# Two queues for the first half of x, and a broadcast copy on two engines, in a two-layer decoder trunk

## The chip, the cores and the metric

The kernel runs on one core of a Trainium2 chip. The time is that of one execution on the device, in microseconds (us). The core has five engines with an instruction stream of their own: PE (TensorE, matrix products), DVE (VectorE), ACT (ScalarE), POOL (GpSimd) and SP (SyncE, which here only issues transfers). PEld is PE's loading of weights. Transfers between the chip's memory (HBM) and the core's SBUF run on 16 DMA engines; an engine that issues one puts it into its own queue and goes on.

## The reference: what is computed

One sequence of 1024 tokens, 1024 wide, goes through two layers and a last norm. Each layer computes

```
mod   = silu(c) @ ada_w[layer] + ada_b[layer]          # shift, scale, gate
h     = rmsnorm(x, norm_g) * (1 + scale) + shift
x     = x + gate * mixer(h)
```

with `rmsnorm(x, g) = x * rsqrt(mean(x*x) + 1e-6) * g` per token. Layer 0's mixer is an input projection, eight heads of sliding-window attention beside eight heads of forgetting attention, a SiLU gate and an output projection. Layer 1's is a projection, a causal convolution of width 4, a gated linear recurrence along the tokens, a SiLU gate and an output projection. The result is `rmsnorm(x, final_g)`. All is float32.

## The kernel before, in words

The kernel keeps x transposed: the 1024 features lie as 8 blocks (k = 0 to 7) of 128 partitions, the tokens along the free dimension, in two halves of 512. For a matmul in float32r each operand is split into a high part (a rounded copy, made by ACT) and a low part (the rest, made by POOL), and a product is three matmuls: high by high, low by high, high by low. Names with `hh`, `whi` are high parts, `hlo`, `wlo` low ones; `ws` are the split weights of the first projection, both parts.

Nearly every instruction goes through a small class, `Queue` (L75), so that the profile gives the helper's line, L85, for all of them; the tiles' names tell them apart. Where an engine's name stands in the set `ordered`, its instructions keep the order in which the program writes them; elsewhere a scheduler orders them. From `ordered |= ALL` (L415) on, the opening is in written order.

The opening, which the change touches:

- SyncE issues `col` (all the small vectors), then x of the first half in five pieces (`load_x(0)`: k = 0-1, 2-3, 4-5 of 512 KB each, then 6 and 7 of 256 KB each), then the rows of `ada` for the shifts and scales and the weights `wg` of the first five gate tiles (`load_block`).
- ACT, DVE and POOL make silu(c) from `col`; POOL spreads it along the free dimension (`vb8`), and PE transposes it into `crow_ps`. ACT loads a table of functions at the start, and another ahead of the square roots.
- `squares(0)`: ACT squares blocks 0, 2, 4, 6 and 7, in this order; DVE squares 1, 3 and 5 and sums pairs (POOL one of them). `norm_sums` adds over the partitions with matmuls against ones (`psq`). Between them PE is given matmuls that compute nothing (`warm`).
- `rstd_of` (L255) makes 1/sqrt of the mean for each token. At that point token t of group i stands on partition t, column i (`v`). The factors have to lie along the tokens on every partition, so they are copied to 128 columns each (`vb`) and PE transposes those blocks of 128 x 128 (`rs`).
- For each of 8 blocks k: two dot products on DVE give the block's scale and shift (`mod_first`), DVE multiplies x by rs and the scale, ACT adds the shift twice (once rounded to `hh`), POOL takes the difference (`hlo`), and PE runs 15 matmuls with the five gate tiles (`pst`): ten with hh, five with hlo. During block 7 ACT also splits `raw_gate`, the weights of a sixth gate tile.

After that comes the rest of layer 0, then layer 1. At the very end the final norm is done for tokens 0 to 511, 512 to 767 and 768 to 1023 in turn; only the last of the three has no matmul left beside it. There `rstd_of` is used again, the transposed factors are also copied by ACT to SBUF (`rsb`) for POOL, and DVE and POOL multiply and SyncE stores.

Of the kernel before, what the change touches and what calls it, by code (L numbers as in the profile page):

```python
# [12 lines left out]
F32 = mybir.dt.float32  # L13
# [11 lines left out]
P = 128  # L25
S = 1024
D = 1024
KT = D // P
HALF = 512
# [19 lines left out]
def hybrid_trunk(  # L49
# [23 lines left out]
    ordered = set()  # L73
# [25 lines left out]
    act, dve, gp = Queue("act", nc.scalar), Queue("dve", nc.vector), Queue("gp", nc.gpsimd)  # L99
# [3 lines left out]
    def copy(out, in_, scale=1.0):  # L103
        act.activation(out, in_, AF.Copy, scale=scale)
# [41 lines left out]
    gp.memset(tiny, 1e-30)  # L146
    tiny2 = const.tile([P, 1], F32, name="tiny2")
    col = const.tile([P, NCOL], F32, name="col")
    sync.dma_start(col, cols)
    nsink = const.tile([P, 8], F32, name="nsink")  # L150
    bfb = const.tile([P, 8], F32, name="bfb")

# [18 lines left out]
        sub(dve, out, l, c)  # L171


    cact = const.tile([P, KT], F32, name="cact")
    ce = const.tile([P, KT], F32, name="ce")
    act.activation(ce, col[:, C_C : C_C + 8], AF.Exp, scale=-1.0)
# [2 lines left out]
    mul(dve, cact, ce, col[:, C_C : C_C + 8])  # L179
    act.activation(tiny2, cact[:, 0:1], AF.Exp)  # L180
    act.activation(tiny2, tiny2, AF.Sqrt)


    l0 = ctx.enter_context(ExitStack())
    gyp = l0.enter_context(tc.tile_pool(name="gyp", bufs=2, reuse_waits="tile"))
    l0a = ctx.enter_context(ExitStack())
    at = l0a.enter_context(tc.tile_pool(name="at", bufs=2, reuse_waits="tile"))

# [3 lines left out]
    def t4(tag, name, dt=F32, bufs=None):  # L192
        bufs = bufs or BUFS[tag]
        return at.tile([P, 1024], dt, tag=tag, name=name, bufs=bufs)

    xh = []
    for h in range(2):
        t = gyp.tile([P, KT, HALF], F32, tag="gy", name=f"x_{h}")
        xh.append(t)

    mm = pe.matmul

# [32 lines left out]
    def norm_sums(sq, w, name, ps=None):  # L235

        psq, steps = sum_steps(sq, w, name, ps)
        for f in steps:
            f()
        return psq  # L240
# [11 lines left out]

        return psq, [lambda n=n, i=i: step(n, i) for n in range(len(sq)) for i in range(w // P)]

    def rstd_of(psq, w, pool, tags, name, ps=None):  # L255

        nt = w // P

        v, t = (psq[:, i * P : i * P + 2 * nt] for i in (1, 2))
        y = pool.tile([P, 8], F32, tag="ny", name=f"ny_{name}", bufs=2)[:, : 2 * nt]  # L260
        dve.tensor_scalar(out=v, in0=psq[:, 0 : 2 * nt], scalar1=1.0 / D, scalar2=EPS, op0=ALU.mult, op1=ALU.add)
        act.activation(y, v, AF.Sqrt)
        dve.reciprocal(y, y)

        dve.scalar_tensor_tensor(out=t, in0=v, scalar=-0.5, in1=y, op0=ALU.mult, op1=ALU.mult)
        mul(dve, t, t, y)
        dve.scalar_tensor_tensor(out=v, in0=t, scalar=1.5, in1=y, op0=ALU.add, op1=ALU.mult)
        vb = pool.tile([P, nt, P], F32, tag=tags[0], name=f"vb_{name}", bufs=2)
        dve.tensor_copy(vb, v.rearrange("p (i two) -> p i two", two=2)[:, :, 0:1].to_broadcast([P, nt, P]))

        def spread():
            prs = (ps or ps_t)(f"rs_{name}")
            for i in range(nt):
                tp(prs[:, i * P : (i + 1) * P], vb[:, i])
            if ps:
                return prs
            rs = pool.tile([P, w], F32, tag=tags[1], name=f"rsb_{name}", bufs=2)
            copy(rs, prs[:, :w])
            return rs, prs

        return spread
# [90 lines left out]
    def start_w(i, k):  # L372
        return tuple(t[:, k % 2, i] for t in four[k // 2]) if i < 4 else tuple(t[:, k] for t in one)

    def load_x(h):
        for k0, k1 in ((0, 2), (2, 4), (4, 6), (6, 7), (7, 8)):
            sync.dma_start(xh[h][:, k0:k1], xT[:, h, k0:k1])

    hl_ada = {}

    parts = {}
# [31 lines left out]
        return sq[0:KT:2]  # L413

    ordered |= ALL  # L415
    load_x(0)
    for c in range(4):
        load_block(c)
    vb8 = at.tile([P, KT, P], F32, tag="P", name="vb8", bufs=NP)
# [13 lines left out]
    psq = norm_sums(sq, HALF, "n0_0", ps_s)  # L433
    mod_first(0, 1)
    warm(WARM)
    spread = rstd_of(psq, HALF, at, ("ptl", "pth"), "n0_0", ps_s)
    mod_first(0, 0)
    split_start(0)
    prs = spread()
# [1115 lines left out]
    for t0, tw in ((0, 512), (512, 256), (768, 256)):  # L1555
# [29 lines left out]
            act.activation(sqs[1], xn[:, KT - 1], AF.Square)  # L1585
        for e in range(KT):
            act.activation(xn[:, e], xn[:, e], AF.Copy, scale=col[:, C_FG + e : C_FG + e + 1])
        spread = rstd_of(norm_sums(sqs, tw, f"n2_{t0}"), tw, xp, ("vb", "rsb"), f"n2_{t0}")
        rs, prs = spread()
        for e in range(KT):  # L1590
            mul(*((gp, xn[:, e], xn[:, e], rs) if e % 4 == 3 else (dve, xn[:, e], xn[:, e], prs[:, :tw])))
# [77 lines left out]
```

## Time and profile before

| what | value |
| --- | --- |
| median of 3 runs | 882.5 us (881.85 to 883.75) |
| profiled execution | 882.07 us, span 880.3 us |
| PE, PEld busy | 857.9, 728.0 us |
| DVE, ACT, POOL busy | 561.5, 536.9, 385.6 us |
| mean granted PE clock | 0.990 |
| first x issue to first projection matmul | 1.19 to 17.03 us |
| last projection matmul group of the opening | 44.33 us |
| last residual add to the last store issue | 869.52 to 874.86 us (first of four stores) |

The span runs from the first to the last instruction; the time around it, 1.8 us, is not in the trace. In a row of the timeline stand the start and the duration in us, the engine, the operation, the tile written and the tiles read, and in brackets how long the engine had been idle and what it waited for. A start is measured from the span's start. SPq and ACTq are the issues of transfers by SyncE and ACT.

### The profile page before, as it was taken

The numbers are of one execution on the slowest core, as the hardware profiler recorded it, in microseconds if no ns is written. First come the engines' busy times: TensorE is split into PE (matmuls) and PEld (weight loads), VectorE is DVE, ScalarE is ACT, GpSimd is POOL, SyncE is SP. The second block draws the span as 40 slices with busy tenths as digits, with TensorE's granted clock in tenths as the row PEclk, the third lists the DMA queues.
The fourth block names the chain that finished last, engine by engine and source line by source line (L and its number), as shares of the span: only waits on it lengthen the run. The fifth ranks groups of instructions, "written<-read, shape, count | busy, mean of one in ns | idle before, by whom it ended". The sixth has DMA issues, their size and how long they took to land.

```text
span 880.3 us, 13493 instructions
## 1 busy us (share of the span) xinstructions
PE 857.9 (97%) x4618; PEld 728.0 (83%) x4618; DVE 561.5 (64%) x1134; ACT 536.9 (61%) x1047; POOL 385.6 (44%) x429
## 2 busy tenths in 40 slices
PE   9999999999989999999999999999999999989995
PEld 8787898888878888888877888878888877868995
DVE  7886657688676566666656668375667655563643
ACT  5765124788685566666666647357767876673532
POOL 4843222334342232232664655532775556585100
PEclk9999999999999999999999999999999999989998
DMA  9944772100113223322373564411221211226042
GB/s 344 403 180 127 218 237 63 47 18 24 37 43 115 87 87 123 123 87 79 118 232 106 176 209 146 141 63 54 79 78 55 71 55 65 86 83 215 14 145 81
DMA packets 54620, 103.83 MB, mean 118 GB/s; under 512 B 6960, under 2 KB 20720, under 8 KB 54040
## 3 DMA queue, kind: packets, MB, share of 16 engines
q1 hardware_dynamic: 53400, 101.93, 35.1%
q10 hardware_dynamic: 1152, 1.05, 0.4%
q8 instruction: 36, 0.59, 0.3%
q14 instruction: 32, 0.26, 0.1%
HBM read 94.02 MB, written 8.93 MB: 117 GB/s over the span
## 4 chain that ended last, share of the span: by engine, by line
PE 77%; issue 6%; POOL 5%; DMA 4%; DVE 3%; ACT 3%; SPq 0%; POOLq 0%; DVEq 0%; ACTq 0%
PE ps_fill L85 23%; PE ps_o L85 10%; PE ps_lx L85 6%; PE pst L85 6%; PE ps_o0c L85 5%; PE ps_lg L85 5%; PE oB L85 4%; PE sB L85 4%; PE ptB L85 4%; PE ps_v L85 3%; DMA ada<-in_ada_dram 2%; PE sA L85 2%; PE oA L85 1%; POOL wlo_lg L85 1%; PE ptA L85 1%
## 5 line engine op out<-in xcount | busy, mean ns | idle before, releaser
L85 PE MATMUL ps_o<-y1h,wo 128*128 128x256 f32 (+1 forms) x336 | 75.2, 318 | 0.0
L85 DVE TENSOR_TENSOR ptl_B<-ptB,pth_B 128x512 fp32r<-128x512 f32 (+1 forms) x80 | 50.9, 636 | 34.7 <-ACT pth_B L85 33.9
L85 ACT ACTIVATE pB<-pB,mnB 128x128 f32<-128x128 f32 (+3 forms) x64 | 49.6, 775 | 32.7 <-DVE mnB L85 26.8
L85 ACT ACTIVATE pth_B<-ptB 128x512 fp32r<-128x512 f32 (+1 forms) x80 | 44.1, 551 | 41.1 <-PE ptB L85 40.2
L85 DVE SCALAR_TENSOR_TENSOR xc_r<-ps_lx,col,xc_r 128x509 f32<-128x509 f32 (+2 forms) x48 | 35.7, 745 | 43.4 <-ACT xt_r L85 42.2
L85 POOL TENSOR_SCALAR_AFFINE_SELECT pB<-pB 128x128 f32<-128x128 f32 x64 | 18.6, 293 | 95.8 <-DMA pB<-gd 88.8
L85 PEld LDWEIGHTS ps_o<-y1h,wo 128*128 128x128 f32 x336 | 56.0, 190 | 4.4
L85 PE MATMUL pst<-hh,ws 128*128 128x512 f32 x192 | 55.5, 397 | 0.0
L85 PE MATMUL ps_o<-y1l,wo 128*128 128x256 f32 (+1 forms) x168 | 53.7, 320 | 0.0
L85 PE MATMUL ps_lg<-h1h,wlo_lg 128*128 128x512 f32 x128 | 50.2, 392 | 0.9 <-POOL wlo_lg L85 0.8
L85 PE MATMUL ps_lx<-h1l,whi_lx 128*128 128x512 f32 x128 | 50.3, 393 | 0.2 <-POOL h1l L85 0.2
L85 PE MATMUL ps_lx<-h1h,wlo_lx 128*128 128x512 f32 x128 | 50.3, 393 | 0.2
L85 PE MATMUL ps_lx<-h1h,whi_lx 128*128 128x512 f32 x128 | 50.3, 393 | 0.0
L85 PE MATMUL ps_lg<-h1l,whi_lg 128*128 128x512 f32 x128 | 49.9, 390 | 0.0
L85 PE MATMUL ps_lg<-h1h,whi_lg 128*128 128x512 f32 x128 | 49.8, 389 | 0.0
L85 POOL TENSOR_TENSOR wlo_lx<-raw_lx,whi_lx 128x512 fp32r<-128x512 f32 x16 | 30.6, 1930 | 43.3 <-ACT whi_lx L85 34.1
L85 ACT ACT_TABLE_LOAD x35 | 44.9, 1283 | 5.1 <-issue 3.0
L85 DVE CUSTOM_DVE_ANT_0 pB<-sB,pB 128x384 f32<-128x384 f32 (+2 forms) x64 | 35.4, 555 | 17.4 <-PE sB L85 10.0
L85 PE MATMUL ptB<-ident,pB 128*128 128x128 f32 x288 | 45.1, 273 | 1.2 <-DVE ptl_B L85 0.7
L85 PEld LDWEIGHTS ptB<-ident,pB 128*128 128x128 f32 x288 | 35.8, 140 | 12.1 <-PE rbT_B L85 1.5
L85 PEld LDWEIGHTS pst<-hh,ws 128*128 128x128 f32 x192 | 35.8, 188 | 9.2 <-issue 0.6
L85 ACT ACTIVATE y1h<-sg_r 128x512 fp32r<-128x512 f32 x16 | 10.0, 632 | 44.9 <-POOL sg_r L85 39.8
(312 smaller groups left out, 2853.5 us busy)
## 6 DMA issues: line engine op xcount, KB each, us to landing
ada<-in_ada_dram SPq DMA_DIRECT2D x32, 512.0 KB
x<-in_xT_dram SPq DMA_DIRECT2D x20, 256.0 KB
ada<-in_ada_dram SPq DMA_DIRECT2D x4, 1024.0 KB
pB<-gd SPq DMA_DIRECT2D x8, 512.0 KB
raw_o0a<-in_wo_dram SPq DMA_DIRECT2D x16, 256.0 KB
raw_o0c<-in_wo_dram SPq DMA_DIRECT2D x16, 256.0 KB
x1d<-x SPq DMA_DIRECT2D x16, 256.0 KB
raw_lx<-in_wl_dram SPq DMA_DIRECT2D x16, 256.0 KB
```

The lines of the kernel that those rows point to most:

```text
L85: ins = issue(*args, **kw)
```

## The change

Three edits, the first two of which belong together.

`col` and x of the first half are issued at one place at the very start, and the five pieces of x are dealt to two queues: ACT issues pieces 1 and 3 (k = 0-1 and 4-5), SyncE pieces 2, 4 and 5. ACT and SyncE keep written order over this piece of the program. The second half's x is still all SyncE's.

In `rstd_of` a new argument `two` halves the copy of the factors: DVE copies the first half of the token groups, ACT the second. It is used for the first half's norm at the opening (4 groups of 128, so 128 x 256 for each engine) and for the last 256 tokens of the final norm (2 groups, 128 x 128 each). The other norms keep the whole copy on DVE.

```
-    sync.dma_start(col, cols)
...
+    xh = [gyp.tile([P, KT, HALF], F32, tag="gy", name=f"x_{h}") for h in range(2)]
+
+    def load_x(h, queues=(sync,)):
+        for i, (k0, k1) in enumerate(((0, 2), (2, 4), (4, 6), (6, 7), (7, 8))):
+            queues[i % len(queues)].dma_start(xh[h][:, k0:k1], xT[:, h, k0:k1])
+
+    ordered |= {"act", "sync"}
+    sync.dma_start(col, cols)
+    load_x(0, (act, sync, act, sync, sync))
...
     act.activation(tiny2, tiny2, AF.Sqrt)
+    ordered.clear()
...
-    def rstd_of(psq, w, pool, tags, name, ps=None):
+    def rstd_of(psq, w, pool, tags, name, ps=None, two=False):
...
-        dve.tensor_copy(vb, v.rearrange("p (i two) -> p i two", two=2)[:, :, 0:1].to_broadcast([P, nt, P]))
+        vs = v.rearrange("p (i two) -> p i two", two=2)[:, :, 0:1]
+        cut = nt // 2 if two else nt
+        dve.tensor_copy(vb[:, :cut], vs[:, :cut].to_broadcast([P, cut, P]))
+        if two:
+            copy(vb[:, cut:], vs[:, cut:].to_broadcast([P, nt - cut, P]))
...
-    load_x(0)
...
-    spread = rstd_of(psq, HALF, at, ("ptl", "pth"), "n0_0", ps_s)
+    spread = rstd_of(psq, HALF, at, ("ptl", "pth"), "n0_0", ps_s, two=True)
...
-        spread = rstd_of(norm_sums(sqs, tw, f"n2_{t0}"), tw, xp, ("vb", "rsb"), f"n2_{t0}")
+        spread = rstd_of(norm_sums(sqs, tw, f"n2_{t0}"), tw, xp, ("vb", "rsb"), f"n2_{t0}", two=t0 == 768)
```

On SyncE, at the start of the program (x_103 and x_91 are the first half's x, before and now; rows of 128x1024 are the 512 KB pieces):

```order
 L85 DMA col<-in_cols_dram 128x144
-L85 DMA x_103<-in_xT_dram 128x1024 x3
-L85 DMA x_103<-in_xT_dram 128x512 x2
+L85 DMA x_91<-in_xT_dram 128x1024
+L85 DMA x_91<-in_xT_dram 128x512 x2
 L85 DMA ada_0_125<-in_ada_dram 128x1024 x2
```

Two of the 512 KB pieces are gone from this queue; `ada` stands two issues nearer to its head.

On ACT, from the first instruction to the split of the first weights, as it stands now (psq holds the factors, raws the weights as loaded, ws their split):

```order
L85 DMA x_91<-in_xT_dram 128x1024 x2
L85 ACT_TABLE_LOAD
L85 ACTIVATE ce<-col 128x8
...
L85 ACTIVATE sq_ptl_1_179<-x_91 128x512
L85 ACTIVATE gsc<-mod,col 128x1
L85 ACTIVATE ny_n_0_217<-psq_n_0_192 128x8
L85 ACTIVATE vb_n_0_224<-psq_n_0_192 128x256
L85 ACTIVATE ws_0_0_115<-raws_0_128 128x512
L85 ACTIVATE ws_0_123<-raw_raws_0_130 128x512
```

New here are the two issues ahead of the table load, and ACT's half of the copy (vb) between the square root (ny) and the split of the first weights. On DVE the copy at the same place is 128x256 instead of 128x512. On PE and POOL every instruction stands where it stood.

On ACT, the last instructions of the program, as they stand now:

```order
L85 ACTIVATE sq_768_9098<-x_768_8861 128x256
L85 ACTIVATE x_768_8861<-x_768_8861,col 128x256
L85 ACTIVATE ny_n_768_9113<-psq_n_768_9108 128x4
L85 ACTIVATE vb_n_768_9120<-psq_n_768_9108 128x128
L85 ACTIVATE rsb_n_768_9126<-rs_n_768_9123 128x256
```

The row vb is new; DVE's copy at this place is 128x128 instead of 128x256.

More of the change, by code (lines that the diff above doesn't have):

```diff
@@ L171, in log1p_exp_neg_abs @@
         sub(dve, out, l, c)
+    l0 = ctx.enter_context(ExitStack())
+    gyp = l0.enter_context(tc.tile_pool(name="gyp", bufs=2, reuse_waits="tile"))
+    xh = [gyp.tile([P, KT, HALF], F32, tag="gy", name=f"x_{h}") for h in range(2)]
[5 more added lines that the diff above has]
+    load_x(0, (act, sync, act, sync, sync))
     cact = const.tile([P, KT], F32, name="cact")
@@ L181, in hybrid_trunk @@
     act.activation(tiny2, tiny2, AF.Sqrt)
-    l0 = ctx.enter_context(ExitStack())
-    gyp = l0.enter_context(tc.tile_pool(name="gyp", bufs=2, reuse_waits="tile"))
+    ordered.clear()
     l0a = ctx.enter_context(ExitStack())
@@ L194, in t4 @@
         return at.tile([P, 1024], dt, tag=tag, name=name, bufs=bufs)
[L196 to L199, printed above, removed]
     mm = pe.matmul
@@ L373, in start_w @@
         return tuple(t[:, k % 2, i] for t in four[k // 2]) if i < 4 else tuple(t[:, k] for t in one)
-    def load_x(h):
-        for k0, k1 in ((0, 2), (2, 4), (4, 6), (6, 7), (7, 8)):
-            sync.dma_start(xh[h][:, k0:k1], xT[:, h, k0:k1])
     hl_ada = {}
```

## The prediction

> **What bounds the kernel now.** I read the page first, for the engine that carries the span and the chain that ended last; then busy time by stretch for the opening 60 us and the timeline of each engine there; then the last 12 us, because the change touches only these two ends.
>
> ```profile
> span 880.3 us, 13493 instructions
> PE 857.9 (97%) x4618; PEld 728.0 (83%) x4618; DVE 561.5 (64%) x1134; ACT 536.9 (61%) x1047; POOL 385.6 (44%) x429
> PE 77%; issue 6%; POOL 5%; DMA 4%; DVE 3%; ACT 3%; SPq 0%; POOLq 0%; DVEq 0%; ACTq 0%
> ```
>
> TensorE (PE) is busy for 97% of the span and is 77% of the last chain. A shift won in the opening therefore passes through the long middle as a shift, and one won behind the last matmul counts directly. The opening, by stretch (the columns are busy time of PE, PE's weight loads, VectorE, ScalarE, GpSimd, then granted clock, DMA share, GB/s):
>
> ```profile
> 1.75:2.50 0.75, 0.75 (x5) 0.75 (x5) 0.00 (x0) 0.26 (x1) 0.00 (x0) 1.00 1.11 180
> 2.50:3.50 1.00, 1.00 (x7) 1.00 (x6) 0.44 (x3) 0.21 (x1) 0.19 (x1) 1.00 0.66 143
> 3.50:8.20 4.70, 4.70 (x34) 4.70 (x34) 2.23 (x4) 3.19 (x6) 2.31 (x2) 1.00 1.02 405
> 12.60:16.00 3.40, 3.40 (x18) 3.36 (x18) 3.14 (x8) 1.22 (x3) 2.50 (x2) 0.50 1.01 376
> 16.00:45.40 29.40, 29.38 (x130) 23.31 (x129) 25.16 (x39) 21.95 (x39) 23.28 (x18) 1.00 1.04 403
> 45.40:60.00 14.60, 14.51 (x72) 11.91 (x70) 12.08 (x16) 7.76 (x13) 6.52 (x5) 1.00 0.36 142
> ```
>
> The DMA engines are full from 3.50 us on and stay at about 400 GB/s to 45.40. So two things run abreast in the opening: a stream of transfers that is never idle once it has started, and the norm chain up to the first projection matmul. Which one sets PE shows at the last of the eight blocks of projection matmuls:
>
> ```profile
> 17.03 2.60 PE L85 MATMUL pst<-hh,ws 128*128 128x512 f32 x10
> 38.73 0.63 ACT L85 ACTIVATE whi_gate<-raw_gate 128x512 fp32r<-128x512 f32 x1 [0.79 <-DMA raw_gate<-in_wt_dram]
> 40.98 0.72 ACT L85 ACTIVATE hh<-x,mod 128x512 fp32r<-128x512 f32 x1 [0.82 <-DVE x L85]
> 41.75 2.20 PEld L85 LDWEIGHTS pst<-hh,ws 128*128 128x128 f32 x10 [0.46 <-ACT hh L85]
> 44.33 1.00 PEld L85 LDWEIGHTS pst<-hlo,ws 128*128 128x128 f32 x5 [0.38 <-POOL hlo L85]
> ```
>
> PE starts the first block at 17.03. At the eighth it waits 0.46 us for hh and 0.38 us for hlo. Both are late because ScalarE (ACT) waited 0.79 us for raw_gate, a transfer, with the split of the last weights and the scale of the block queued behind it. So at 45 us the transfers have overtaken the norm chain: PE has 0.84 us of slack there against its own start, and what counts at the end of the opening is how much earlier the stream of transfers runs.
>
> **The change, part by part.** It removes no arithmetic. Two of the five x transfers of the first half move from SyncE's queue to the head of ScalarE's, and half of two copies moves from VectorE (DVE) to ACT.
>
> *Issue of x.*
>
> ```profile
> 0.73 0.40 SPq L85 DMA_DIRECT2D col<-in_cols_dram  x1
> 1.19 2.59 SPq L85 DMA_DIRECT2D x<-in_xT_dram  x5
> 3.82 0.94 SPq L85 DMA_DIRECT2D ada<-in_ada_dram  x2
> L679 ACTq DMA_DIRECT2D bias<-rd x8: 310/432/606, 129.4 to 134.2; - x8
> ```
>
> SyncE issues col at 0.73 and the first x at 1.19; five x issues take 2.59, 0.52 each. On ACT a transfer's issue takes 432 ns in the median (310 to 606; the bias transfers of this trace). In the change ACT issues the first x as its first instruction, at 0.73, which is 1.19 - 0.73 = 0.46 earlier, and its second at about 1.2. SyncE has three x left and reaches the first ada at about 1.19 + 3 x 0.52 = 2.75 instead of 3.82, so it stays ahead of the engines.
>
> How much earlier does the full stream start? Bounds: nothing, if the slow second from 2.50 to 3.50 (143 GB/s) is not made by the order of issues. At most, the stream would be full from 1.75 on: 0.75 x (1 - 180/405) + 1.00 x (1 - 143/405) = 0.42 + 0.65 = 1.06 us. I take 0.46, the offset of the issue, since the bytes behind the first x are the same and the engines are full once x flows.
>
> *When x lands, and the norm chain.*
>
> ```profile
> 5.38 0.63 ACT L85 ACTIVATE sq<-x 128x512 f32<-128x512 f32 x1
> 6.66 0.63 ACT L85 ACTIVATE sq<-x 128x512 f32<-128x512 f32 x1 [0.65 <-DMA x<-in_xT_dram]
> 7.96 0.63 ACT L85 ACTIVATE sq_pth<-x 128x512 f32<-128x512 f32 x1 [0.67 <-DMA x<-in_xT_dram]
> 8.63 1.29 ACT L85 ACTIVATE sq_ptl<-x 128x512 f32<-128x512 f32 x2
> 5.39 0.69 DVE L85 TENSOR_TENSOR sq<-x 128x512 f32<-128x512 f32 x1 [1.78 <-DMA x<-in_xT_dram]
> 10.17 0.69 DVE L85 TENSOR_TENSOR sq_ptl<-sq_ptl,sq_ptl 128x512 f32<-128x512 f32 x1
> ```
>
> The squares follow the landings: 5.38, 6.66 and 7.96 lie 1.3 apart, and 512 KB at 405 GB/s is 1.29. If the five pieces still land in their order, all is 0.46 earlier; ACT ends its squares at 9.92 - 0.46 = 9.46 and DVE's last sum begins near 9.7 in place of 10.17. If the two queues share the engines by halves, the pieces 2 (ACT), 4 and 5 (SyncE) overlap: piece 2 lands not at 7.96 - 0.46 = 7.50 but shortly before the last one, near 8.7, while the last byte of x still lands 0.46 earlier. ACT takes the squares in order, so three of them (0.655 each with the gap) then run from 8.7 to 10.65, and the last sum begins near 10.7: 0.5 later than before. So the first block starts between 0.46 earlier and 0.5 later.
>
> The Trainium skill ("DMA: Bandwidth & Descriptors", sections "Queues, rings and completion order" and "Issuing engines are not separate DMA queues") speaks for the halves, and against this change: the queues of the two engines sit on the same 16 DMA engines, which serve them in turn packet by packet, so that a second issuer saves only its time of issue. By that rule the stream still gains the 0.46 of issue, and the norm chain is the 0.5 later; no row read here shows two queues busy at once.
>
> Both cases give nearly the same end. In order: PE's own arrival at the eighth block is 41.75 - 0.46 - 0.46 = 40.83, raw_gate lands 0.46 earlier, so the block starts 0.46 earlier. By halves: PE arrives at 41.29 + 0.5 = 41.79. ACT's chain ahead of raw_gate ended at 38.73 - 0.79 = 37.94, now 38.44, so whi_gate starts 0.29 earlier and hlo with it. PE reaches the hlo matmuls at 43.95 + 0.5 - 0.46 = 43.99, finds hlo at 44.33 - 0.29 = 44.04, and is 0.29 ahead. **Term: -0.3 to -0.46; I take -0.4.** Behind it PE is busy for 14.51 of 14.60 us, and raw_gate's successors move with the stream.
>
> *ACT pays for its issues.*
>
> ```profile
> 0.73 1.28 ACT L85 ACT_TABLE_LOAD   x1 [0.73 <-PEq L1658]
> 2.75 0.21 ACT L85 ACTIVATE ce<-col 128x8 f32<-128x8 f32 x1 [0.74 <-DMA col<-in_cols_dram]
> 3.67 1.04 POOL L85 COPY vb<-cact 128x1024 f32<-128x1024 f32 x1 [0.70 <-DVE cact L85]
> 6.12 1.04 PE L85 MATMUL crow_ps<-ident,vb 128*128 128x128 f32 x8
> ```
>
> The table load moves from 0.73 to about 1.65 and ends at 2.93, past col's landing (2.73), so ce and the chain behind it are 0.2 late (0.55 with issues of 606 ns). Waiting on it: the eight crow transposes at 6.12, whose input was ready at 4.71 (1.4 of cover), and ACT's first square, 5.38 + 0.2 = 5.58, while it sat 0.65 + 0.67 idle between its squares. Cost nothing; without the cover, 0.2 to 0.55.
>
> *The split copy at the front.*
>
> ```profile
> 13.57 0.69 DVE L85 COPY vb_n<-psq_n 128x512 f32<-128x512 f32 x1
> 14.18 1.27 DVE L85 CUSTOM_DVE_ANT_0 ada<-ada,crow_ps,col 128x1024 f32<-128x1024 f32 x1
> 15.47 0.75 DVE L85 SCALAR_TENSOR_TENSOR x<-rs_n,gsc,x 128x512 f32<-128x512 f32 x1
> 12.57 0.62 ACT L85 ACTIVATE ws<-raws 128x512 fp32r<-128x512 f32 x1
> 16.25 0.72 ACT L85 ACTIVATE hh<-x,mod 128x512 fp32r<-128x512 f32 x1 [2.31 <-DVE x L85]
> 13.27 1.27 POOL L85 TENSOR_TENSOR ws<-raws,ws 128x512 fp32r<-128x512 f32 x1 [5.76 <-ACT ws L85]
> 12.11 2.46 PE L85 MATMUL warm<-ones 128*128 128x128 f32 x12
> 14.37 1.07 PE L85 MATMUL rs_n<-ident,vb_n 128*128 128x128 f32 x4
> 872.39 0.42 DVE L85 COPY vb_n<-psq_n 128x256 f32<-128x256 f32 x1
> ```
>
> Half of 128x512 is 128x256, which took 0.42 at the tail: DVE is free 0.27 earlier. But the transposes of the factors (rs) stand behind twelve warm-up rows on PE, whose clock is at half there, and end at 15.44 whenever the copy ends; x needs them. So between 0 and -0.27 at PE's start; I take 0, and the slack at the eighth block would swallow it. ACT now waits for v with the splits of the first weights behind it: ws<-raws from 12.57 to about 14.0, both splits done by 15.3, inside the 2.31 that ACT idled ahead of hh. GpSimd's part of them (1.27 each) starts at 14.7 in place of 13.27 and ends near 16.0 and 17.3; PE needs the first at 17.03 and the second nine matmuls on. Cost nothing.
>
> *The split copy at the tail.*
>
> ```profile
> 871.36 0.17 ACT L85 ACTIVATE ny_n<-psq_n 128x4 f32<-128x4 f32 x1 [0.36 <-DVE psq_n L85]
> 872.96 0.66 PE L85 MATMUL rs_n<-ident,vb_n 128*128 128x128 f32 x2 [1.84 <-DVE vb_n L85]
> 873.66 0.38 ACT L85 ACTIVATE rsb_n<-rs_n 128x256 f32<-128x256 f32 x1 [2.13 <-PE rs_n L85]
> ```
>
> Here PE waits for the copy and ACT is idle. DVE's half: between 0.17 (four columns) and 0.42, so 0.29. ACT's half: between 0.17 and 0.38, so 0.28. The two run abreast: 0.42 - 0.29 = 0.13 gained. Bounds: -0.25 (a half at the price of four columns), and nothing if ACT's half starts so late that it ends where the whole copy ended. **Term: -0.13.**
>
> **Sum:** -0.4 - 0.13 = -0.5 us on the profiled execution (882.07 us, span 880.3): 881.5. That execution lies 0.43 under the median of the three runs, 882.5; on the median's scale it is 882.0, which I forecast. 0.2% of this time, about what a measurement can tell from no change, is 1.76 us; the forecast lies inside it.
>
> **Rivals.**
> 1. *Nothing at the front.* The stream starts no earlier, since the slow second belongs to the first transfers, whoever issues them. For it: 143 GB/s stood there although SyncE had issued three x by 2.75. Against it: the first x itself moves by 0.46. Only the tail is left: 882.4.
> 2. *The whole ramp is gained.* Two issuers fill the engines from 1.75 on and the norm chain follows: -1.06 - 0.13 = -1.2, 881.3. Against it: the norm chain would need pieces in order, or the slack of 0.84.
> 3. *Slower: the clock at the first block.* The granted clock is 0.50 from 12.60 to 16.00 and full again only 1.03 us ahead of 17.03. If the start of the norm sums shifts so that the half clock holds for one more such stretch of 3.4 us from PE's start, PE loses half of it, 1.7; the slack takes 0.84; with the tail it is +0.73: 883.2. It decides from 1.7 us of half clock behind the first block's start; two stretches would be +2.4, 884.9. Against it: the matmuls and warm-up rows keep their order. "TensorE: Matmul & The Clock Gate" of the Trainium skill (the section on the HAM clock gate) has the gate judge in free-running windows of about 3.4 us; the length agrees with the 3.40 here.
>
> **How the numbers follow.** Forecast 0.50; rival 1 0.27; rival 2 0.14; rival 3 0.09. Their middles run from 881.3 to 883.2; three runs of one kernel scattered from 881.85 to 883.75, -0.65 and +1.25, of which a median keeps about half. That makes 880.8 to 883.1. Faster by over 0.2% (under 880.7) needs rival 2 with a low draw or a gain I do not see: 0.10. Slower (over 884.3) needs rival 3 with two stretches: 0.04. Within: 0.86.
>
> **What would show it.** Right: SyncE's first ada issue near 2.75, the stream at 400 GB/s from about 3.0, raw_gate's split near 38.3 to 38.45, the hlo matmuls of the eighth block, at 44.33, near 44.0, and at the tail 0.29 in place of 0.42 for DVE's copy, with rs that much sooner behind it. The landing order is read from ACT's third square: 7.5 in order, about 8.7 by halves. Wrong: a first block more than 0.9 later than 17.03, a granted clock under 1 behind it, ACT's table load past 2.2, or a shift at 45 us that is gone by 860.

## The result, and the profile after

Over 22 executions of each, the kernel before took 882.34 us in the median (881.50 to 884.19) and the changed kernel 883.43 us (881.93 to 885.10). The ratio is 1.0012, with a 95% interval of 1.0006 to 1.0017: the change costs about 1.1 us. That lies inside the 0.2% within which I counted no change, but on the side that I did not forecast, above the range (forecast 882.0, range 880.8 to 883.1).

In the timeline of the changed kernel the issues moved as forecast: SyncE's first `ada` at 2.74 in place of 3.82. What waits for `col` moved too.

```profile
0.74 0.40 SPq L85 DMA_DIRECT2D col<-in_cols_dram  x1
1.20 1.50 SPq L85 DMA_DIRECT2D x<-in_xT_dram  x3
2.74 1.13 SPq L85 DMA_DIRECT2D ada<-in_ada_dram  x2
0.73 0.91 ACTq L85 DMA_DIRECT2D x<-in_xT_dram  x2
1.67 1.28 ACT L85 ACT_TABLE_LOAD   x1 [1.67 <-PEq L1662]
4.34 0.21 ACT L85 ACTIVATE ce<-col 128x8 f32<-128x8 f32 x1 [1.38 <-DMA col<-in_cols_dram]
```

`col` was issued at 0.74, as before, but ACT's first use of it starts at 4.34 instead of 2.75. The table load is not the reason: it ended at 2.95, and ACT waited 1.38 us more for the transfer. POOL's first use of it came as late (4.37). In the kernel before, `col` had the engines nearly to itself until the first x, issued 0.46 us behind it, began to move; now a 512 KB piece of x from the other queue starts with it, and the 72 KB of `col` land 1.6 us later. (The DMA records have `col`'s packets from 1.77 to 2.38 us and x's first at 2.24 in the kernel before; now `col`'s from 1.76 to 3.82 and x's from 1.90.)

The stretch 2.50 to 3.50 in the windows view (last column GB/s) shows the other side, 312 GB/s where it was 143:

```profile
2.50:3.50 1.00, 1.00 (x7) 1.00 (x6) 0.00 (x0) 0.45 (x1) 0.00 (x0) 1.00 0.83 312
```

The late `col` runs down the whole norm chain, in the timelines of the changed kernel's engines:

```profile
6.74 0.99 PEld L85 LDWEIGHTS crow_ps<-ident,vb 128*128 128x128 f32 x8 [0.42 <-POOL vb L85]
6.85 1.14 ACT L85 ACTIVATE sq<-x 128x512 f32<-128x512 f32 x2
10.79 0.69 DVE L85 TENSOR_TENSOR sq_ptl<-sq_ptl,sq_ptl 128x512 f32<-128x512 f32 x1
14.19 0.42 DVE L85 COPY vb_n<-psq_n 128x256 f32<-128x256 f32 x1
14.71 0.38 ACT L85 ACTIVATE vb_n<-psq_n 128x256 f32<-128x256 f32 x1 [1.42 <-DVE vb_n L85]
17.69 2.56 PE L85 MATMUL pst<-hh,ws 128*128 128x512 f32 x10
```

PE now waits for `vb` where the transposes had 1.4 us of cover. ACT's first square, behind the second table load, starts at 6.85 instead of 5.38, the last sum at 10.79 instead of 10.17, and the first block at 17.69 instead of 17.03: 0.66 us late. The two halves of the copy do not run abreast: ACT's starts at 14.71, when DVE's has ended at 14.61.

Yet at the eighth block this execution has lost nearly nothing. First two rows of the kernel before, then the changed kernel's:

```profile
45.59 0.39 PE L85 MATMUL pst<-hh,whi_gate 128*128 128x512 f32 x1
60.03 0.42 PEld L85 LDWEIGHTS rs_n<-ident,vb_n 128*128 128x128 f32 x4 [0.56 <-issue]
```

```profile
38.54 0.63 ACT L85 ACTIVATE whi_gate<-raw_gate 128x512 fp32r<-128x512 f32 x1 [0.77 <-DMA raw_gate<-in_wt_dram]
41.97 2.30 PEld L85 LDWEIGHTS pst<-hh,ws 128*128 128x128 f32 x10
44.31 1.12 PEld L85 LDWEIGHTS pst<-hlo,ws 128*128 128x128 f32 x5
45.70 0.39 PE L85 MATMUL pst<-hh,whi_gate 128*128 128x512 f32 x1
59.84 0.42 PEld L85 LDWEIGHTS rs_n<-ident,vb_n 128*128 128x128 f32 x4 [0.28 <-issue]
```

PE's waits of 0.46 and 0.38 us, now at 41.97 and 44.31, are gone, so this slack of 0.84 us paid for all but 0.11 of the 0.66 (45.70 against 45.59). At 60 us this execution is 0.2 us ahead, and its span is 880.9 us against 880.3. So in this execution the late start is made good, and 0.8 us are lost behind 60 us. Two waits stand there that the kernel before does not have (PEld's timeline of the changed kernel):

```profile
111.83 0.19 PEld L85 LDWEIGHTS ps_v<-wvl,hh 128*128 128x128 f32 x1 [0.62 <-POOL wvl L85]
344.21 0.31 PEld L85 LDWEIGHTS ptB<-ident,pB 128*128 128x128 f32 x3 [0.79 <-ACT pB L85]
```

The first is for the low parts of two weight tiles on POOL, which took 4.34 us where they took 3.67. Ahead of the second, POOL begins another such pair at 337.69 instead of 336.19. Why POOL is late at these places is not shown. The experiments below are about the opening; what their traces say of these two waits stands at their end.

At the tail, ACT's half again starts when DVE's ends, but each is short and PE transposes the first half meanwhile. From the copy's start to ACT's `rsb` it is 874.28 - 873.23 = 1.05 us, in place of 873.66 - 872.39 = 1.27:

```profile
873.23 0.29 DVE L85 COPY vb_n<-psq_n 128x128 f32<-128x128 f32 x1
873.56 0.28 ACT L85 ACTIVATE vb_n<-psq_n 128x128 f32<-128x128 f32 x1 [1.18 <-DVE vb_n L85]
874.28 0.38 ACT L85 ACTIVATE rsb_n<-rs_n 128x256 f32<-128x256 f32 x1 [0.45 <-PE rs_n L85]
```

But the two executions had different clocks there. The windows of the kernel before, of the changed kernel and of e7 (whole copies, below) show it in the third number from the end; e7's copy and `rsb` stand under them:

```profile
872.80:873.70 0.90, 0.66 (x2) 0.29 (x2) 0.01 (x1) 0.04 (x1) 0.00 (x0) 0.50 0.00 0
873.20:874.00 0.80, 0.33 (x2) 0.25 (x2) 0.29 (x1) 0.28 (x1) 0.00 (x0) 1.00 0.00 0
873.50:874.60 1.10, 0.41 (x2) 0.20 (x2) 0.45 (x2) 0.03 (x1) 0.00 (x0) 1.00 0.00 0
873.55 0.42 DVE L85 COPY vb_n<-psq_n 128x256 f32<-128x256 f32 x1
874.57 0.38 ACT L85 ACTIVATE rsb_n<-rs_n 128x256 f32<-128x256 f32 x1 [1.87 <-PE rs_n L85]
```

At full clock the whole copy takes 874.57 - 873.55 = 1.02 us, no more than the halves. The 0.22 us are the clock's. Where the clock is halved for most of the transposes, the halves take 1.15 (e15) and 1.17 (e12) against 1.27, a gain of at most about 0.1.

### The profile page after: what moved, and what is told of

The parts are those of the page before. It is cut to its first block, busy times and chain, and to the rows that moved or that the text cites. A ratio compares the mean times of both kernels' runs of the same rounds, so it can differ in the third digit from the quotient of the medians.

```text
span 880.9 us, 13496 instructions
## 1 busy us (share of the span) xinstructions
PE 858.2 (97%) x4618; PEld 729.0 (83%) x4618; DVE 559.3 (63%) x1134; ACT 537.2 (61%) x1049; POOL 386.4 (44%) x429
## 4 chain that ended last, share of the span: by engine, by line
PE 49%; POOL 5%; issue 4%; ACT 2%; DVE 1%; DMA 0%; POOLq 0%; DVEq 0%
PE ps_o L85 11%; PE ps_fill L85 9%; PE ps_lx L85 6%; PE ps_lg L85 6%; PE ps_o0c L85 5%; PE oB L85 3%; PE ptB L85 3%; PE sB L85 2%; POOL wlo_lg L85 1%; POOL wlo_lx L85 1%; POOL wrl_r L85 1%; PE psr L85 1%; PE ps_o0b L85 1%; PE psi L85 1%; ACT h1h L85 1%
## 5 line engine op out<-in xcount | busy, mean ns | idle before, releaser
L85 PEld LDWEIGHTS ptB<-ident,pB 128*128 128x128 f32 x288 | 35.7, 140 | 12.6 <-ACT pB L85 1.9
```

The costliest lines, as they stand in the source:

```text
L85: ins = issue(*args, **kw)
```

## Experiments

All ratios are against the kernel before, run beside it on the same chip. The tail is the number of executions whose span is over 1.5 us above the median span of the kernel before on that chip; the kernel before itself has 4 of 151.

| kernel | median, us | before, us | ratio (95%) | tail |
| --- | --- | --- | --- | --- |
| e1 two queues alone | 882.72 | 881.67 | 1.0013 (1.0004 to 1.0022) | 2 of 11 |
| e2 both split copies alone | 882.27 | 881.67 | 1.0005 (0.9996 to 1.0014) | 0 of 11 |
| e3 `col` behind 1 piece, one queue | 882.52 | 881.67 | 1.0009 (1.0000 to 1.0018) | 1 of 11 |
| e4 changed kernel | 882.46 | 881.67 | 1.0011 (1.0003 to 1.0020) | 4 of 11 |
| e5 ACT issues one later piece | 883.78 | 882.17 | 1.0016 (1.0006 to 1.0026) | 6 of 12 |
| e6 `col` behind 2 pieces, one queue | 884.70 | 882.17 | 1.0028 (1.0017 to 1.0040) | 6 of 6 |
| e7 new text, old order | 882.14 | 882.17 | 1.0001 (0.9992 to 1.0009) | 0 of 11 |
| e8 tail copy alone | 881.98 | 882.17 | 0.9997 (0.9988 to 1.0006) | 0 of 11 |
| e9 late split | 882.02 | 881.96 | 1.0005 (0.9997 to 1.0014) | 2 of 11 |
| e10 changed + late split | 883.57 | 881.96 | 1.0016 (1.0008 to 1.0025) | 6 of 11 |
| e11 three more empty matmuls | 882.13 | 881.96 | 1.0005 (0.9996 to 1.0014) | 3 of 11 |
| e12 late split + tail | 881.97 | 881.96 | 1.0004 (0.9995 to 1.0012) | 1 of 12 |
| e13 changed + wide sums | 881.84 | 881.90 | 0.9999 (0.9990 to 1.0008) | 0 of 11 |
| e14 wide sums | 882.12 | 881.90 | 1.0002 (0.9993 to 1.0010) | 1 of 11 |
| e15 changed kernel | 882.55 | 881.90 | 1.0005 (0.9997 to 1.0014) | 0 of 11 |
| e16 twelve empty matmuls fewer | 883.47 | 881.90 | 1.0020 (1.0011 to 1.0029) | 7 of 11 |
| e17 changed + wide + late split | 881.59 | 881.63 | 0.9998 (0.9989 to 1.0007) | 0 of 11 |
| e18 wide + late split + tail | 882.92 | 881.63 | 1.0015 (1.0005 to 1.0024) | 4 of 11 |

The first theory was A: `col` is late because it shares the DMA engines with the first piece of x, and its chain makes the loss. The rivals: the split copies (B), the chance of how later transfers fall against the engines, with the loss at 108 to 112 and 328 to 337 us (C), and the second queue by itself (A'). In the last runs the letters H and C have another meaning, which the texts give.

### Which edit: e1, e2, e8, e7, and the changed kernel again (e4)

e1 is the changed kernel with whole copies, e2 the changed kernel with one queue, e8 the same with only the tail's copy halved, e7 with both edits undone in the new text:

```
e1, e7, e8:
-    spread = rstd_of(psq, HALF, at, ("ptl", "pth"), "n0_0", ps_s, two=True)
+    spread = rstd_of(psq, HALF, at, ("ptl", "pth"), "n0_0", ps_s)
e1, e7:
-        spread = rstd_of(norm_sums(sqs, tw, f"n2_{t0}"), tw, xp, ("vb", "rsb"), f"n2_{t0}", two=t0 == 768)
+        spread = rstd_of(norm_sums(sqs, tw, f"n2_{t0}"), tw, xp, ("vb", "rsb"), f"n2_{t0}")
e2, e7, e8:
-    load_x(0, (act, sync, act, sync, sync))
+    load_x(0)
```

> The changed kernel with both copies of the norm's factors whole on VectorE again; x of the first half still comes through two queues. Theory A (col): the small vectors (col) share the DMA engines with the first piece of x, land at 4.3 instead of 2.7 us, and the silu chain, ScalarE's squares and GpSimd's pair sum follow, so the first projection matmul is 0.6 us late. Then this kernel has all of the loss: +1.1 to +1.4 us against the kernel before, col's landing near 4.3, first block near 17.7 to 17.9. Rival B (copies): the second half of the copy waits for the first, ScalarE's splits of the first weights start 2.4 us late and GpSimd's with them; then this kernel is at 0 or up to 0.4 us faster. Rival C (chance of phase: the loss arises at 108 to 112 us and at 328 to 337 us, from the phase of transfers against the engines): any time between -0.4 and +1.1, and other places of loss in its trace.

> The kernel before with the two split copies alone; col and x all on SyncE's queue as before. Theory A: -0.2 to -0.3 us, all of it at the tail (residual add to the end 10.78 to about 10.53 us), and the first block within 0.3 us of 17.03. Rival B: +0.8 to +1.1 us, with the splits of the first weights late on ScalarE and GpSimd and a wait of PE for them or for hlo. Rival C: between -0.3 and +0.6.

> The changed kernel once more, for a second trace. All theories: +0.6 to +1.5 us. Theory A: col's landing (first ACTIVATE ce) again past 4 us and the first block again 0.5 us or more late. Rival C: the steps of the loss at 108 to 112 and 328 to 337 us are gone or lie elsewhere; theory A with a loss that PE's slack does not swallow would show a shift already at 46 us.

> The kernel before with the copy split at the tail alone. Theory A: -0.2 us (the tail from the last residual add to the end 0.2 to 0.25 us shorter, as in the changed kernel, although ScalarE's half waits for VectorE's), which this comparison can hardly tell from nothing. Rival B (the copies cost): +0.3 us or more.

> A control: the changed kernel's text with both edits undone, col and the five pieces of x on SyncE in their old order. Every engine has the instructions of the kernel before in the same order; only the place in the text differs. All theories: 0, within 0.4 us. What it is away from 0 is what this comparison does to two equal kernels.

The two queues alone cost 1.05 us, as much as the whole change beside them (0.79). The tail's copy alone is 0.2 us below the kernel before, inside the interval; by the rows above it is worth nothing at full clock. The new text in the old order is level. The copies together came out at +0.6 with an interval that holds zero, so B is not excluded by e2 itself; e13 and e17 below hold both copies and lose nothing. The loss comes with the queues.

e2's profile has `col` on time (first use at 2.69), and yet its first block starts at 18.17. PE's clock was halved from 10.8 to 17.6 us, twice as long as in the kernel before (windows and PE timeline of e2):

```profile
10.80:17.60 6.80, 6.80 (x34) 6.80 (x34) 4.57 (x12) 2.33 (x6) 1.97 (x2) 0.50 1.03 367
18.17 1.17 PE L85 MATMUL pst<-hh,ws 128*128 128x512 f32 x4
```

So the doubled stretch comes without a second queue too. There it was made good: rs of the second half's norm stands at 60.08, and at 60.03 in the kernel before.

### Is it col: e3, e6, e5

All three have whole copies. In e3 and e6 SyncE issues everything, with `col` behind one or two pieces of x; e5 has two queues, with ACT's table load (by an Exp of a constant) written first and only the third piece issued by ACT:

```
e3 (e6: two pieces ahead of col):
+    sync.dma_start(xh[0][:, 0:2], xT[:, 0, 0:2])
     sync.dma_start(col, cols)
-    load_x(0, (act, sync, act, sync, sync))
+    for k0, k1 in ((2, 4), (4, 6), (6, 7), (7, 8)):
+        sync.dma_start(xh[0][:, k0:k1], xT[:, 0, k0:k1])
e5:
+    act.activation(tiny2, tiny, AF.Exp)
     sync.dma_start(col, cols)
-    load_x(0, (act, sync, act, sync, sync))
+    load_x(0, (sync, sync, act, sync, sync))
```

> The kernel before (one queue, whole copies) with col issued behind the first piece of x instead of ahead of it: the first piece is issued 0.46 us earlier, col 0.46 us later and behind 512 KB in the same queue. Theory A: col lands at 4 us or later, crow's transposes and ScalarE's squares are late as in the changed kernel, the first block starts 0.4 to 0.8 us late, and the time is +0.3 to +1.1 us. If col's lateness is not the cause: within 0.2 us of the kernel before, or 0.3 us faster for the earlier x.

> One queue, whole copies, col behind the first two pieces of x: a larger dose of the delay alone. Theory A with slack: col lands near 6 us, the first block is 2 to 3 us late, and the loss of the time is that less the slack of the opening (0.84 us less what is used): +1.2 to +2.2 us. If the opening has no slack in the typical execution, the loss is the whole delay of the first block: +2 to +3 us. If col's delay is not what costs the time: under +0.8 us.

> Two queues again, whole copies, but ScalarE loads its table first (a one-column Exp) and only then, near 2.2 us, issues one piece of x, the third; col and the other four pieces stay with SyncE, so nothing shares the DMA engines with col. Theory A (col late): col lands near 2.7 as before, the first block is within 0.3 us of its place before, and the time is within 0.4 us of the kernel before. Theory A' (a second queue hurts by itself, by interleaving the pieces): col on time, but ScalarE's third square later than 7.96 by 0.3 us or more and the time +0.5 to +1.1 us.

ACT's timelines of e3, then e6, then e5:

```profile
4.62 0.21 ACT L85 ACTIVATE ce<-col 128x8 f32<-128x8 f32 x1 [2.60 <-DMA col<-in_cols_dram]
```

```profile
6.03 0.21 ACT L85 ACTIVATE ce<-col 128x8 f32<-128x8 f32 x1 [4.01 <-DMA col<-in_cols_dram]
```

```profile
0.73 1.28 ACT L85 ACT_TABLE_LOAD   x1 [0.73 <-PEq L1663]
1.15 0.40 ACTq L85 DMA_DIRECT2D x<-in_xT_dram  x1
2.72 0.21 ACT L85 ACTIVATE ce<-col 128x8 f32<-128x8 f32 x1 [0.49 <-DMA col<-in_cols_dram]
6.56 0.63 ACT L85 ACTIVATE sq<-x 128x512 f32<-128x512 f32 x1 [1.18 <-DMA x<-in_xT_dram]
```

With one queue and `col` at 4.62, 0.28 us later than in the changed kernel, the loss is 0.85 us, with an interval that begins at no change; at 6.03 it is 2.5. So a late `col` costs time by itself, and more of it costs more. e3's profiled execution, like the changed kernel's, makes its late first block (17.72) good: its rs is at 59.95. e5 missed its aim and told more for it: ACT issued its piece at 1.15, during the table load, and not behind it. `col` then came on time (2.72), but the third piece ran abreast with the first, which landed 1.2 us late (6.56 against 5.38), and the loss was 1.6 us. What the second queue delayed was each time what is needed first: `col` in the changed kernel, the first piece of x in e5. The Trainium skill ("DMA: Bandwidth & Descriptors", section "Issuing engines are not separate DMA queues") has the transfers of all issuers interleave on the same 16 engines. These rows agree, with 1.6 and 1.2 us.

### Does PE's lateness pass to the end: e9, e10, e11, e12

Theory S was the prediction's: the slack at the eighth block swallows what PE is late. Theory N: it does not, in most executions.

e9 and e11 are the kernel before with one edit each, e10 is the changed kernel with the late split, e12 e9 with the tail's halves in two tiles:

```
e9, e10, e12 (and e17, e18 below):
-        if c in (5, 6):
-            ws[0] += half_of(graw[NS][c - 5])
+        if c == 6:
+            ws[0] += half_of(graw[NS][0]) + half_of(graw[NS][1])
e11, behind prs = spread():
-    warm(WARM)
+    warm(WARM + 3)
e12 (and e18), for the tail's ACT half:
-            copy(vb[:, cut:], vs[:, cut:].to_broadcast([P, nt - cut, P]))
+            vb2 = pool.tile([P, nt - cut, P], F32, tag="vb2", name=f"vb2_{name}", bufs=1)
+            copy(vb2, vs[:, cut:].to_broadcast([P, nt - cut, P]))
```

> The kernel before with one thing moved: ACT's split of the first half of raw_gate stands behind the eighth block's hh in place of ahead of it, so that neither hh nor hlo of that block queues behind the transfer's wait. No transfer moves, no work goes. Theory S (the opening's end is the later of the transfers and the norm chain, and the transfers win by the 0.84 us that PE waits at the eighth block): those 0.46 + 0.38 waits go, the sixth gate tile's first matmul comes at about 44.75 in place of 45.59, and the time falls by 0.6 to 0.84 us. Theory N (what that profile shows at the eighth block is one execution's; in the typical one PE itself is the last to come there): no change, 0 to -0.2 us.

> The changed kernel with the same move of the raw_gate split. With the transfer's wait taken from the eighth block, only the norm chain and PE's own clock decide its start. Theory S: the changed kernel's lateness of 0.66 us at the first block, until now swallowed, shows in full against the same move without the change: 0.66 less 0.2 for the tail, so about 0.45 us above the run of the move alone, and 0.2 to 0.4 us below the kernel before. Theory N: the changed kernel loses its 1 us wherever the split stands: 0.8 to 1.1 us above the kernel before.

> The kernel before with three more matmuls that compute nothing ahead of the first block of projection matmuls (nine in place of six): PE starts the block 0.64 us later (3 x 0.21, from 12 rows in 1.89 us at mostly full clock, two rows each), at about 17.7 as in the changed kernel, with no transfer and no other engine touched. Theory S: the slack of 0.84 us at the eighth block swallows it: 0 to +0.1 us. Theory N: it passes to the end: +0.6 us, about what the late col alone and the two queues alone have cost.

> A candidate: the kernel before with the raw_gate split moved behind the eighth block's hh, and the tail's copy halved over two tiles of their own, so that ACT's half need not wait for DVE's. Theory S: -0.6 to -0.84 at the opening and -0.3 at the tail (the two halves of 0.29 abreast, 0.42 - 0.29 = 0.13, and one transpose overlapped), about -1.0 us. Theory N: the tail alone, -0.3 us.

Rows of e9 (PE, DVE and PEld timelines):

```profile
44.90 0.39 PE L85 MATMUL pst<-hh,whi_gate 128*128 128x512 f32 x1
40.79 2.39 DVE L85 TENSOR_TENSOR sq<-x 128x512 f32<-128x512 f32 x2 [1.43 <-DMA x<-in_xT_dram]
53.45 0.30 PEld L85 LDWEIGHTS psq_n<-ones,sq_pth 128*128 128x128 f32 x2 [1.10 <-DVE sq_pth L85]
59.90 0.44 PEld L85 LDWEIGHTS rs_n<-ident,vb_n 128*128 128x128 f32 x4 [0.20 <-issue]
```

The split's move did at the eighth block what was expected (44.90 in place of 45.59), and the time did not fall: DVE, now early, waits 1.43 us for the second half's x, PE waits 1.10 us for DVE's sums at 53.45, and rs stands at 59.90, where it stood before (60.03). There is a second place bound by transfers behind the first, which I had not looked for.

e11 delayed PE alone and nothing else. Its median rose by 0.17 us, against 0.6 by theory N, but 3 of its 11 executions lie 1.6 us or more above the kernel before. e10 is the same on a larger scale: 3 executions within 0.2 us of the kernel before, 8 from 1.3 us up. Neither S nor N gives such a spread. e10's profiled execution (span 881.8) is one of the upper group, and its PE timeline and windows (PE's clock is the third number from the end) show what made it late:

```profile
15.81 1.06 PE L85 MATMUL rs_n<-ident,vb_n 128*128 128x128 f32 x4
16.66 2.48 PE L85 MATMUL warm<-ones 128*128 128x128 f32 x12
18.90 1.39 PE L85 MATMUL pst<-hh,ws 128*128 128x512 f32 x5
...
12.00:15.50 3.50, 3.50 (x17) 3.50 (x18) 2.29 (x9) 0.98 (x4) 0.00 (x0) 0.50 1.00 366
...
17.00:19.00 2.00, 2.00 (x13) 2.00 (x12) 2.00 (x4) 1.27 (x2) 1.57 (x2) 0.57 1.01 399
```

The stretch of clock 0.50 lasts 6.8 us here, from 11.9 to 18.7, not 3.4 us as in the profile of the kernel before. The factors' transposes and the empty matmuls behind them run at half speed, and the first block starts at 18.90: 1.87 us later than before, more than the slack holds. Here rs is late too, at 60.80.

With every execution its mean clock is listed. Up to 0.991 and above it, the kernel before lies on average at +0.29 (97 executions) and -0.22 us (54) from its median; the kernels with two queues dealt as in the change (e1, e4, e10, e15) lie at +1.46 (26) and +0.29 (18). Their mean clock is the same, 0.9913 and 0.9914. So the clock is not lower in the changed kernel; its executions with a low clock lie 1.2 us above its others, those of the kernel before 0.5.

That cannot be put down to the opening alone. The mean is over the whole span, and nearly every profile has a second stretch of half clock near 775 us, of 6.8 us in some and 3.4 in others (windows of the kernel before, then of e4):

```profile
773.80:780.60 6.80, 5.33 (x13) 4.18 (x14) 4.48 (x5) 5.30 (x8) 6.80 (x5) 0.50 0.24 77
774.50:777.80 3.30, 3.30 (x9) 2.52 (x9) 3.06 (x4) 1.90 (x5) 3.30 (x2) 0.50 0.31 96
```

### Taking the half clock away, and forcing it: e13, e14, e15, e16

e13 is the changed kernel and e14 the kernel before, both with 64 columns of ones in the opening's norm sums (`nc_` is 64 there, 2 elsewhere; `rstd_of` reads every 64th pair). e16 is the kernel before with less for PE to do between the sums and the first block:

```
e13, e14:
-                psq[:, 2 * i : 2 * i + 2], sq[n][:, i * P : (i + 1) * P], ones[:, 0:2],
+                psq[:, nc_ * i : nc_ * (i + 1)], sq[n][:, i * P : (i + 1) * P], ones[:, 0:nc_],
e16:
     mod_first(0, 1)
-    warm(WARM)
     spread = rstd_of(psq, HALF, at, ("ptl", "pth"), "n0_0", ps_s)
...
     prs = spread()
-    warm(WARM)
     modulate_in(0, 0, prs)
```

> The changed kernel, with the opening's norm sums against 64 columns of ones in place of 2: the same 32 matmuls and weight loads (about 0.115 us each, set by the loads), the same sums, each written 64 times instead of twice, so that TensorE's array is not nearly idle through that stage. Theory H (the loss is the halved clock that follows the nearly idle stage, in those executions in which it reaches the first block of projection matmuls, which is late by the late col): the opening's stretch of clock 0.50 goes or shortens, executions more than 1.5 us above the kernel before become rare, and the median falls by 0.6 to 1.0 us, to within 0.3 us of the kernel before. Theory C (col's lateness costs its 0.7 us by itself, whatever the clock): no change against the changed kernel, +0.7 to +1.1 us.

> The same wider sums in the kernel before (its instruction order, one queue, whole copies). Theory H: the stretch goes here too, but it cost little, since the slack at the eighth block swallowed it: 0 to -0.3 us. Theory C: 0.

> The changed kernel once more, on the chip of the three others: +0.7 to +1.1 us against the kernel before, a third of its executions more than 1.5 us above. Theory H: if the profiled execution is one of these, its granted clock is 0.50 past the start of the first block; if it is one near the kernel before, the stretch ends ahead of it.

> The kernel before without the twelve matmuls that compute nothing between the norm sums and the first block (two groups of six), so that TensorE is idle there; the first block's inputs are ready at the same time, about 17.0 us, and no transfer moves. Theory H: the halved clock reaches well past the first block's start in most executions, one window of 3.4 us there costs 1.7 us, of which the slack takes up to 0.84: +0.9 us and more, with a tail like the changed kernel's. Theory C: nothing that the norm chain waits for is later, 0.

Windows of e13, with its ACT and PE rows; then the same of e16:

```profile
12.00:15.50 3.50, 3.10 (x29) 2.90 (x27) 2.83 (x10) 0.57 (x2) 0.00 (x0) 1.00 1.00 370
...
5.19 0.21 ACT L85 ACTIVATE ce<-col 128x8 f32<-128x8 f32 x1 [2.25 <-DMA col<-in_cols_dram]
18.09 2.60 PE L85 MATMUL pst<-hh,ws 128*128 128x512 f32 x10 [0.35 <-ACT hh L85]
```

```profile
17.00:19.00 2.00, 1.51 (x4) 1.22 (x5) 2.00 (x4) 1.96 (x4) 0.73 (x1) 0.50 1.02 411
19.00:21.00 2.00, 2.00 (x6) 1.59 (x5) 2.00 (x6) 1.16 (x2) 1.80 (x2) 0.50 1.04 415
...
17.49 4.30 PE L85 MATMUL pst<-hh,ws 128*128 128x512 f32 x10 [1.60 <-ACT hh L85]
```

With the wider sums the clock stays at 1.00 through the opening, in this profile and in those of e14, e17 and e18. The changed kernel is then level with the kernel before, with no execution in the tail, although `col` came at 5.19 in the profiled one, later than in any other profile of it. All 22 executions of e13 and e17 have a clock above 0.991. In the kernel before the wider sums change nothing, as H expects. e16 changes no transfer and nothing of the norm chain's work; PE is idler, the clock is halved from 11.0 to 21.2 us, and the loss is 1.6 us: its first ten matmuls take 4.30 us instead of 2.60, 1.7 us more.

Four reserves. On this chip the changed kernel itself (e15) lost only 0.65 us, and its interval meets e13's; what supports the step most is e10 against e17, the same kernel without and with the wider sums, at 1.0016 (1.0008 to 1.0025) and 0.9998 (0.9989 to 1.0007), though on two chips. And of the six profiled executions with `col` or x delayed by a second queue and sums of two columns (the first profile after, e1, e4, e5, e10, e15) only e10's shows the doubled stretch, and e2's shows it without them, so the profiles do not say that it comes more often with the change. e3 had no half clock in the opening with sums of two columns. And three of e18's executions, with the wider sums, list a clock of 0.988 and lie 2.4 to 3.0 us above the kernel before, so the wider sums do not keep the clock up in every execution.

### Is the earlier stream worth anything: e17, e18

e17 is e13 with the late split; e18 is e12 with the wider sums, so one queue:

> The changed kernel with the wider sums and the late split of raw_gate. If the earlier stream is worth its 0.2 to 0.5 us once nothing else decides: rs of the second half's norm at 59.4 to 59.8 (60.06 before) and the time 0.4 to 0.7 us below the kernel before, tail included. If the late col's chain still decides: level with the kernel before, -0.2 to +0.2 us.

> One queue, col on time, wider sums, late split, the tail's halves on two tiles of their own. The second half's norm stays bound by the second half's x, which comes at the old time: rs at 59.9 to 60.1. The tail gives its 0.3 us: -0.2 to -0.4 us against the kernel before. If the stream sets the opening's end, e17 is ahead of it there by 0.2 to 0.5 us.

The rs of the second half's norm, in PEld's timelines of e17 and then e18:

```profile
59.49 0.42 PEld L85 LDWEIGHTS rs_n<-ident,vb_n 128*128 128x128 f32 x4 [0.28 <-issue]
```

```profile
54.15 0.30 PEld L85 LDWEIGHTS psq_n<-ones,sq_pth 128*128 128x128 f32 x2 [1.40 <-DVE sq_pth L85]
60.60 0.43 PEld L85 LDWEIGHTS rs_n<-ident,vb_n 128*128 128x128 f32 x4 [0.21 <-issue]
```

With two queues, rs comes at 59.49 and the wait for the second half's sums is gone; with one it comes at 60.60, and the time is 1.33 us longer. The earlier stream is real. But e17 is only level with the kernel before, so no combination tried beats it by more than can be measured, and e18's loss of 1.3 us is larger than I can explain: e12 has the same late split without the wider sums and lost nothing. That stays open, and an unexplained loss of this size also weakens what e10 and e17 say of the wider sums.

Behind 60 us there is more to see in the same traces. There are seven profiles with the queues as changed: the first one, e1, e4, e10, e13, e15 and e17. All but e10's have that rs between 59.20 and 60.00, none later than the kernel before (60.03). From there to the end of the span the seven take 820.8 to 821.4 us, the kernel before 820.2; the kernels with one queue and `col` on time take 820.2 to 821.5, seven of ten under 820.7. The wait for `wvl` at about 112 us stands in four of the seven (first, e10, e15, e17; 0.57 to 0.64 us); in kernels with one queue it is 0.27 at most (e9, e12). The wait at about 344 us stands in five (first, e1, e10, e13, e17; 0.40 to 0.84) and, of the kernels with one queue, in e7 alone (0.85). e4 has neither.

This is what rival C of e1 and e4 expected: both waits come and go between executions. They stand in more of the profiles with two queues, and no run takes them away, so how the 1.1 us divide between the opening and these places is open.

## Why the prediction was wrong

- **"ACT pays for its issues ... cost nothing": the step that failed.** The sum took `col`'s landing as fixed at 2.73 and only moved the table load, which did go to 1.67 as computed. `col` landed 1.6 us later, because a piece of x from the other queue ran beside it. The 1.4 us of cover at the transposes and ACT's idle time between squares were used up, and the first block came 0.66 us late. With one queue a late `col` alone cost 0.85 us (4.62, an interval from no change up) and 2.5 (6.03). I had the sharing of the engines in hand, weighed it for the pieces of x against each other, and not for `col`, the smallest transfer and the first one needed.
- **"The slack at the eighth block would swallow it": right in the profile, not in every execution.** The half clock of the opening differs in length and place from execution to execution (12.6 to 16.0 in the profile of the kernel before, 11.9 to 18.7 in e10, 10.8 to 17.6 in e2, none in e3), and a longer one needs the same 0.84 us. With `col` late and the doubled stretch, e10 was late past 60 us; with the doubled stretch alone, e2 was not. That the other slow executions of the changed kernel are like e10 is argued, not shown. Rival 3, to which I gave 0.09 and 883.2 us, is near the measured 883.43 partly by luck: its half clock behind the start of the first block stands in no profile of the changed kernel (17.31 against 17.69; in e10 18.7 against 18.90). In e10 the half clock is on the rows ahead of the block.
- **"A shift won in the opening therefore passes through the long middle as a shift": not in this profile.** It was 0.2 us ahead at 60 us and 0.6 behind at the end, with the waits of 0.62 and 0.79 us at 111.83 and 344.21 between. The working named a shift that is gone by 860 as a sign that it is wrong, and priced no wait behind 60 us.
- **The stream, "-0.3 to -0.46; I take -0.4".** It started earlier (312 GB/s from 2.50 to 3.50), and `raw_gate`'s split came 0.19 us earlier in the first profile (38.73 to 38.54). At 60 us the profile was 0.2 ahead, half of the term. In the profiles it shows most where the second half's x is what PE waits for (e17 against e18).
- **When x lands: neither case as given.** The third square came at 7.89, the pieces no longer set the pace: ACT's first square waited for the second table load behind `col`, and its squares then ran without a wait.
- **"The two run abreast": wrong, and no loss.** ACT's half begins when DVE's ends, at both places. Both read the factors from one PSUM tile. In e12, whose halves are written to two tiles, ACT still begins at 872.94, when DVE's has ended at 872.90:

```profile
872.61 0.29 DVE L85 COPY vb_n<-psq_n 128x128 f32<-128x128 f32 x1
872.94 0.28 ACT L85 ACTIVATE vb_n<-psq_n 128x128 f32<-128x128 f32 x1 [1.19 <-DVE vb_n L85]
```

  So it is not the tile written. The Trainium skill ("PSUM — Partial Sum Buffer", section "PSUM bank collisions raise a hardware error") says that two engines may not touch one bank at the same partitions at once, reads included, and that the compiler's scheduler puts a dependency between them. The order here agrees with it; a copy from another bank was not tried. At the front nothing came of the halves that the runs can tell. At the tail I had 0.13 from two halves abreast; at full clock the rows give nothing (1.05 against 1.02 for the whole copy), at half clock at most about 0.1.
- **"That makes 880.8 to 883.1": the sum does not come out.** The middles run up to 883.2, and half of the scatter of 1.25 on top makes 883.8. The range stopped below its own highest middle; the measured 883.43 lies within what its terms give.

## What to carry to other kernels

A second queue on the same DMA engines took time from the transfer that was needed first, so let a small early one land before another queue starts anything large; ask of every row's landing, not only of the moved one's, what runs beside it. Slack that one profile shows may already be in use in other executions: compare the spread and the clock of many executions before spending it. Look behind the place that was changed: this profile had made the late start good by 60 us and lost its time after that. And compare two rows only with the clock of each beside them; the gain read at the tail was a difference of clock.

## What the runs showed of the hardware

- 128 x 144 of float32 (72 KB) came into use 1.6 us later when a 512 KB transfer was issued on another queue at the same moment (first use at 4.34 against 2.75; 5.19 in e13).
- ACT issued a transfer during its table load (e5: issue at 1.15, load from 0.73 to 2.01).
- Thirty-two norm-sum matmuls with 64 columns took as long as with 2 (the first 16 rows 1.90 against 1.85 us), and in all four profiles with 64 (e13, e14, e17, e18) the granted clock stayed at 1.00 through the opening. In 15 of the 16 profiles with 2 columns it fell to 0.50 there; e3 is the exception.
- The half clock of the opening came in pieces of 3.4 us or about twice and three times that (11.9 to 18.7 in e10, 11.0 to 21.2 in e16). That agrees with the windows of 3413 ns in the Trainium skill's "TensorE: Matmul & The Clock Gate", section on the HAM clock gate.
- The same copy and transposes at the tail took 1.02 us at clock 1.00 (e7) and 1.27 at 0.50 (the kernel before).
